# Moving the sum of squares of a second norm from TensorE to VectorE, and the scalings of its first half behind the projection

## The chip, the cores and the metric

One core of a Trainium2 chip runs the whole kernel. The metric is the device time of one execution in microseconds (us). The engines are named as the profile names them: PE is TensorE (PEld its weight loads), DVE is VectorE, ACT is ScalarE, POOL is GpSimd, SP issues the DMAs.

## What is computed

One inference step of a decoder layer, for 1024 prompt tokens and 64 sample tokens (1088 columns in all) and a model width of 1024. Cut to what matters here:

```
def rms_norm(x, g):
    xf = x.astype(jnp.float32)
    y = xf * lax.rsqrt(jnp.mean(xf * xf, axis=-1, keepdims=True) + EPS)
    return (y * g.astype(jnp.float32)).astype(x.dtype)
...
    x = x + jnp.concatenate([a, o], axis=-1) @ w_out
    h = rms_norm(x, norm_ffn_g)
    g_full = jnp.concatenate([ffn_past, h @ w_ffn_gate], axis=1)
    g = depthwise_conv_valid(g_full, ffn_conv_w, ffn_conv_b)
    x = x + (jax.nn.silu(g) * (h @ w_ffn_up)) @ w_ffn_down
```

The change lies between the first and the third of the last five lines: the end of the output projection, the norm of its result, and the operands of the feed-forward products.

## The kernel before

Everything is stored transposed: a tile holds 128 channels on the partitions and the 1088 tokens along the row. Float32 products are made of three fp32r products each: an operand is split into a high part (copied by ACT with rounding) and a low part (the rest, by a subtraction), and high x high, low x high and high x low are added up in PSUM (lines 840, 842 and 843 in the stage here).

**The last part of the output projection** (`out_half`, line 940). The projection is summed over four groups of input tiles; the last group has two tiles (`mx`, split into `mh` and `ml`, lines 858 to 864) and its weights are split into `wh` and `wl` (lines 865 to 876; `wl` on POOL, line 874). The 1088 columns are worked in two halves of 544 (`HN`). For each half, the loop runs over the eight output tiles m: `block_product` makes 12 products of 272 columns into a PSUM pair; DVE adds the pair to the residual tile `x2[m]` (line 949, called the residual addition here), SP writes that half tile to DRAM, ACT squares it (line 952), and PE sums the squares over the partitions by five products with a column of ones (line 955), all eight tiles into the one PSUM pair `ss`.

**The norm** (`norm_half`, `rstd`, line 182). From `ss`, DVE and ACT make the reciprocal root with one Newton step (`rv`, `rr`, `rt`, lines 193 to 206), PE spreads it over the partitions by five transposes (line 213), ACT copies it to `rb` (line 215). `scale` (line 960) multiplies a half tile by it. The root of the first half is made while the second half is projected.

**The feed-forward operands.** The feed-forward products use a seven-product block scheme: the blocks are the quarters of the input and their sums and differences, each split into high and low by `split` (line 880: ACT the high part, DVE the low). Block b11 is tiles 0 to 3 of the first half, b21 tiles 4 to 7 of the first half, b22 tiles 4 to 7 of the second; t1 to t4 are differences. The first products of the stage are px (b11, then b21), pv (b22), pz (t3), py (t2, t1).

**What sets the order.** Each engine works through its own queue in order. The queues are filled by a scheduler at build time, from dependences and its own guess of durations; `tc.issue_after(x)` holds an instruction back, in that order, until x. While the projection runs, the weights of the first feed-forward product are prepared too: `weight_parts` (line 899: ACT the high part, POOL the low part, line 903) and four additions on DVE (lines 918 to 921).

The rings that matter: `pair` hands out four PSUM pairs, of which `ss` holds one during a half.

## Time and profile before

| | |
|---|---|
| time, median of 3 runs | 1442.53 us (1441.99 to 1445.53) |
| profiled execution: its own time | 1442.15 us |
| profiled execution: its span | 1440.2 us |
| busy in the span: PE, DVE, ACT, POOL | 1368.0, 846.8, 515.5, 436.8 us |

The span runs from the first to the last instruction of the profiled execution; all times of the rows below are counted from its start. The execution's own time holds 1.95 us more, around the span. The stage that the change touches lies between 602 and 694 us. A row of the timeline gives the start, the time, the engine, the line of the kernel, the operation, its output and inputs, and how often it follows itself; in brackets how long the engine sat idle before it and what ended that. PEclk is the granted share of TensorE's full clock of 2.4 GHz: 1.00 is 2.4 GHz, 0.50 is 1.2 GHz.

### The profile page before, as it was taken

The numbers are of one execution on the slowest core, as the hardware profiler recorded it, in microseconds if no ns is written. First come the engines' busy times: TensorE is split into PE (matmuls) and PEld (weight loads), VectorE is DVE, ScalarE is ACT, GpSimd is POOL, SyncE is SP. The second block draws the span as 40 slices with busy tenths as digits, with TensorE's granted clock in tenths as the row PEclk, the third lists the DMA queues.
The fourth block names the chain that finished last, engine by engine and source line by source line (L and its number), as shares of the span: only waits on it lengthen the run. The fifth ranks groups of instructions, "written<-read, shape, count | busy, mean of one in ns | idle before, by whom it ended". The sixth has DMA issues, their size and how long they took to land.

```text
span 1440.2 us, 25005 instructions
## 1 busy us (share of the span) xinstructions
PE 1368.0 (95%) x10151; PEld 1298.0 (90%) x10151; DVE 846.8 (59%) x1631; ACT 515.5 (36%) x982; POOL 436.8 (30%) x307
## 2 busy tenths in 40 slices
PE   7989999999999989896999999999999999999995
PEld 7989888999977768896999999999999899999995
DVE  7398695566574566538755667556566742423146
ACT  5312111457564564235433233333323431212033
POOL 3221112110010016220554455454445312224124
PEclk9999999999999998988999999999999999999997
DMA  7237676756698795330022222122222481414003
GB/s 269 59 133 269 216 266 187 193 155 181 168 290 248 222 251 178 129 115 32 30 90 76 76 90 68 53 91 91 75 76 91 144 312 45 137 48 130 12 9 116
DMA packets 84883, 195.17 MB, mean 136 GB/s; under 512 B 12576, under 2 KB 46752, under 8 KB 84768
## 3 DMA queue, kind: packets, MB, share of 16 engines
q1 hardware_dynamic: 84768, 193.57, 42.6%
q8 instruction: 80, 1.31, 0.4%
q14 instruction: 35, 0.29, 0.1%
HBM read 145.03 MB, written 48.52 MB: 134 GB/s over the span
## 4 chain that ended last, share of the span: by engine, by line
PE 77%; DVE 11%; DMA 6%; issue 2%; POOL 1%; ACT 1%; SPq 1%; POOLq 0%; DVEq 0%; ACTq 0%
PE g L174 9%; PE g L172 9%; PE g L173 9%; PE py L840 4%; PE py L842 4%; PE py L843 4%; DVE cacc L333 4%; PE o L666 3%; PE s L581 3%; PE pz L842 3%; PE pz L843 3%; PE pz L840 3%; PE px L843 3%; PE px L840 3%; PE px L842 3%; PE t L649 2%
## 5 line engine op out<-in xcount | busy, mean ns | idle before, releaser
L148 POOL TENSOR_TENSOR wl<-wr,wh 128x768 fp32r<-128x768 f32 (+2 forms) x61 | 116.7, 1915 | 462.1 <-PE g L174 391.1
L172 PE MATMUL g<-xh,wh 128*128 128x384 f32 (+1 forms) x472 | 158.6, 336 | 0.0
L174 PE MATMUL g<-xh,wl 128*128 128x384 f32 (+1 forms) x472 | 157.1, 333 | 0.0
L173 PE MATMUL g<-xl,wh 128*128 128x384 f32 (+1 forms) x472 | 157.0, 333 | 0.0
L172 PE MATMUL g<-ah,wh 128*128 128x384 f32 (+1 forms) x432 | 141.1, 332 | 4.2 <-ACT wh L146 3.2
L173 PE MATMUL g<-al,wh 128*128 128x384 f32 (+1 forms) x432 | 143.4, 332 | 1.5 <-DVE al L1135 1.5
L174 PE MATMUL g<-ah,wl 128*128 128x384 f32 (+1 forms) x432 | 143.0, 332 | 0.5 <-POOL wl L148 0.5
L146 ACT ACTIVATE wh<-wr 128x768 fp32r<-128x768 f32 (+2 forms) x62 | 52.0, 839 | 236.2 <-PE g L174 173.9
L903 POOL TENSOR_TENSOR s<-wr,s 128x1024 fp32r<-128x1024 f32 x44 | 107.2, 2438 | 85.0 <-ACT s L902 43.2
L1157 DVE TENSOR_TENSOR x<-g,x 128x384 f32<-128x384 f32 (+1 forms) x72 | 38.0, 534 | 136.8 <-PE g L174 136.6
L622 ACT ACTIVATE y<-y,m 128x128 f32<-128x128 f32 (+1 forms) x192 | 88.4, 463 | 32.6 <-DVE m L610 32.5
L174 PEld LDWEIGHTS g<-xh,wl 128*128 128x128 f32 x472 | 89.7, 190 | 2.3 <-issue 2.1
L172 PEld LDWEIGHTS g<-xh,wh 128*128 128x128 f32 x472 | 90.0, 191 | 1.4 <-issue 1.2
L173 PEld LDWEIGHTS g<-xl,wh 128*128 128x128 f32 x472 | 90.1, 191 | 1.1 <-issue 1.0
L585 DVE CUSTOM_DVE_ANT_0 y<-s,pmk 128x128 f32<-128x128 f32 (+1 forms) x192 | 63.9, 379 | 43.2 <-PE s L581 35.8
L172 PEld LDWEIGHTS g<-ah,wh 128*128 128x128 f32 x432 | 81.7, 190 | 5.0 <-ACT wh L146 3.6
L173 PEld LDWEIGHTS g<-al,wh 128*128 128x128 f32 x432 | 81.9, 190 | 2.1 <-DVE al L1135 2.1
L174 PEld LDWEIGHTS g<-ah,wl 128*128 128x128 f32 x432 | 82.0, 190 | 0.9 <-POOL wl L148 0.9
L333 DVE SCALAR_TENSOR_TENSOR cacc<-gp,prm,cacc 128x1024 f32<-128x1024 f32 x60 | 80.1, 1334 | 0.1
L1086 DVE SCALAR_TENSOR_TENSOR fc<-gb,prm,fc 128x1104 f32<-128x1104 f32 x44 | 78.9, 1813 | 2.0 <-ACT fc L1084 1.2
L903 POOL TENSOR_TENSOR wa<-wr,wa 128x1024 fp32r<-128x1024 f32 (+1 forms) x23 | 56.1, 2442 | 61.9 <-ACT wa L902 61.9
L381 DVE TENSOR_TENSOR qkv<-g,rb 128x384 f32<-128x384 f32 (+1 forms) x53 | 41.1, 776 | 47.1 <-PE g L174 47.0
(304 smaller groups left out, 4147.0 us busy)
## 6 DMA issues: line engine op xcount, KB each, us to landing
cr<-in_kc SPq DMA_DIRECT2D x24, 768.0 KB, 8.3
cr<-in_vc SPq DMA_DIRECT2D x24, 768.0 KB, 7.5
kk<-dk SPq DMA_DIRECT2D x48, 256.0 KB, 7.6
u<-u SPq DMA_DIRECT2D x22, 544.0 KB, 3.0
ur<-u SPq DMA_DIRECT2D x22, 544.0 KB, 5.0
wr<-in_w_in SPq DMA_DIRECT2D x22, 512.0 KB, 4.9
wr<-in_w_gate SPq DMA_DIRECT2D x22, 512.0 KB, 3.3
wr<-in_w_up SPq DMA_DIRECT2D x22, 512.0 KB, 4.7
```

Source lines behind the costliest of these rows:

```text
L148: lo_eng.tensor_sub(lo, raw, hi.bitcast(F32))
L172: nc.tensor.matmul(ps[c], whi[:, k, :], xh[:, t0:t0 + n], start=(k == 0), stop=False)
L173: nc.tensor.matmul(ps[c], whi[:, k, :], xl[:, t0:t0 + n], start=False, stop=False)
L174: nc.tensor.matmul(ps[c], wlo[:, k, :], xh[:, t0:t0 + n], start=False, stop=(k == nk - 1))
L333: eng.scalar_tensor_tensor(acc[:, :S], gp[:, j:j + S], col(w0 + j), acc[:, :S], op0=ALU.mult, op1=ALU.add)
L585: nc.vector.tensor_tensor_reduce(out=y[:, o:o + n], in0=ps[:, o:o + n], in1=mask, op0=ALU.add, op1=ALU.min, scale=1.0, scalar=3e38, accum_ ...
L622: nc.scalar.activation(y, y, AF.Exp, bias=m[:, 4 * g + i:4 * g + i + 1], scale=-1.0, accum_out=den[:, g, 2 * hd + u, i:i + 1])
L840: nc.tensor.matmul(ps, whi[:, k, :], xh[:, t], start=(start and k == 0), stop=False, skip_group_check=True)
L842: nc.tensor.matmul(ps, whi[:, k, :], xl[:, t], start=False, stop=False, skip_group_check=True)
L843: nc.tensor.matmul(ps, wlo[:, k, :], xh[:, t], start=False, stop=(k == nk - 1), skip_group_check=True)
L903: nc.gpsimd.tensor_sub(lo, x, hi.bitcast(F32))
L1086: nc.vector.scalar_tensor_tensor(c[:, :W], gb[i][:, t:t + W], col(C_FW + 3 * f + t), c[:, :W], op0=ALU.mult, op1=ALU.add)
```

## The change

Three edits. (1) The squares of a half are no longer summed by PE over the partitions tile by tile: DVE adds the eight squared tiles into the first (`acc`), and PE sums the partitions once, by five products with ones in `rstd` (line 191 of the changed kernel). (2) All scalings and splits of the first half (b11 and b21) are held back behind the last residual addition; those of b21 behind the last step of the second half's root (`rooted`). The first half's norm is called after tile 3 of the second half, not after tile 2. (3) The low parts `wl` of the last group's weights are made by DVE, not by POOL (line 874).

```
-        def rstd(sq, div, new, width=N, sums=None):
+        rooted = [None]
+        def rstd(sq, div, new, width=N):
+            ps = bank(*rbank[0])
...
-            ps = sums
-            if ps is None:
-                ps = bank(*rbank[0])
-                for i, n in enumerate(size):
-                    nc.tensor.matmul(ps[:n, i:i + 1], sq[:, i * P:i * P + n], ones, start=True, stop=True)
+            for i, n in enumerate(size):
+                nc.tensor.matmul(ps[:n, i:i + 1], sq[:, i * P:i * P + n], ones, start=True, stop=True)
...
-            nc.vector.scalar_tensor_tensor(r, t, 1.5, r, op0=ALU.add, op1=ALU.mult)
+            rooted[0] = nc.vector.scalar_tensor_tensor(r, t, 1.5, r, op0=ALU.add, op1=ALU.mult).ins
...
-                nc.gpsimd.tensor_sub(lo, r, hi.bitcast(F32))
+                nc.vector.tensor_sub(lo, r, hi.bitcast(F32))
...
-            sums = pair("ss")
             for m in range(KT):
...
                 s = slot("t1", "sq", F32)
                 nc.scalar.activation(s, x, AF.Square)
-                for i in range(0, HN, P):
-                    w = min(P, HN - i)
-                    nc.tensor.matmul(sums[:w, i // P:i // P + 1], s[:, i:i + w], ones, start=(m == i == 0),
-                                     stop=(m == KT - 1), skip_group_check=True)
+                if m == 0:
+                    acc = s
+                else:
+                    added = nc.vector.tensor_add(acc, s, acc).ins
                 hook(m, added)
-            return sums, added
+            return acc, added
...
-        def first_blocks(m, added):
-            if m == 2:
-                r0.append(norm_half(sums0))
-            if m >= 4:
-                with tc.issue_after(added):
-                    scale(0, m - 4, r0[0])
-                    split(x2[m - 4][:, :HN], "b11", m - 4)
-
-        sums1, added = out_half(1, first_blocks)
-        r1 = norm_half(sums1)
-        for k in range(4):
-            with tc.issue_after(added):
-                scale(0, k + 4, r0[0])
-            split(x2[k + 4][:, :HN], "b21", k)
+        def norm_first(m, added):
+            if m == 3:
+                r0.append(norm_half(sq0))
+
+        def first_blocks(k, tag, after):
+            for i in range(k, k + 4):
+                with tc.issue_after(after):
+                    scale(0, i, r0[0])
+            for i in range(k, k + 4):
+                with tc.issue_after(after):
+                    split(x2[i][:, :HN], tag, i - k)
+
+        sq1, added = out_half(1, norm_first)
+        r1 = norm_half(sq1)
+        first_blocks(0, "b11", added)
+        first_blocks(4, "b21", rooted[0])
```

Outside the stretch between the last group of the projection and the first feed-forward products, the order of every engine stays as it was. Inside it, three places matter.

PE, around the root of the first half (g with a number above 6700 is a PSUM pair of the projection, ss the sums of squares, rr the root, sq a squared tile). Before, the last ones of the first half, where the second half has begun:

```order
L955 MATMUL ss_6701<-ones,sq_6871 128x1 x4
L955 MATMUL ss_6701<-ones,sq_6871 32x1
L955 MATMUL ss_6878<-ones,sq_6894 128x1 x4
L955 MATMUL ss_6878<-ones,sq_6894 32x1
L840 MATMUL g_6901<-mh_6628,wh_6640 128x272
```

and, 24 products later, the transposes of the root:

```order
L843 MATMUL g_6923<-mh_6634,wl_6645 128x272
L213 MATMUL g_1282_6957<-ident,rr_6949 128x128 x4
L213 MATMUL g_1283_6963<-ident,rr_6949 128x32
L955 MATMUL ss_6878<-ones,sq_6916 128x1 x4
L955 MATMUL ss_6878<-ones,sq_6916 32x1
L840 MATMUL g_6966<-mh_6628,wh_6644 128x272
```

Now, behind the 48th product of the second half (its tile 3):

```order
L843 MATMUL g_6897<-mh_6634,wl_6645 128x272
L191 MATMUL g_1278_6915<-ones,sq_6716 128x1 x4
L191 MATMUL g_1278_6915<-ones,sq_6716 32x1
L213 MATMUL g_1283_6933<-ident,rr_6925 128x128 x4
L213 MATMUL g_1284_6939<-ident,rr_6925 128x32
L840 MATMUL g_6942<-mh_6628,wh_6650 128x272
```

Fourteen of the sixteen sums with ones are gone, and no product stands between the ones of the first half and the transposes of its root.

DVE in the same place (x is a residual tile, rv, rr and rt the steps of the root). Before:

```order
L949 TENSOR_TENSOR x_1148_6214<-g_6856,x_1148_6214 128x544
L949 TENSOR_TENSOR x_1099_5934<-g_6879,x_1099_5934 128x544
L195 TENSOR_SCALAR rv_6945<-ss_6701 128x4
L198 TENSOR_SCALAR rv_6945<-ss_6701 32x1
L200 RECIPROCAL rr_6949<-rv_6945 128x5
L204 TENSOR_TENSOR rt_6952<-rr_6949 128x5
```

Now (sq_6716 is the sum of the first half, sq_6859 that of the second):

```order
L948 TENSOR_TENSOR x_1113_6014<-g_6879,x_1113_6014 128x544
L955 TENSOR_TENSOR sq_6716<-sq_6841,sq_6716 128x544
L948 TENSOR_TENSOR x_1120_6054<-g_6897,x_1120_6054 128x544
L955 TENSOR_TENSOR sq_6859<-sq_6876,sq_6859 128x544
L195 TENSOR_SCALAR rv_6921<-g_1278_6915 128x4
L198 TENSOR_SCALAR rv_6921<-g_1278_6915 32x1
L955 TENSOR_TENSOR sq_6859<-sq_6894,sq_6859 128x544
L200 RECIPROCAL rr_6925<-rv_6921 128x5
L955 TENSOR_TENSOR sq_6859<-sq_6912,sq_6859 128x544
L204 TENSOR_TENSOR rt_6928<-rr_6925 128x5
```

From the first residual addition to the root's last step, DVE's queue now holds 12 residual additions, 10 additions of squares, 2 splits `ml`, the 4 additions of lines 918 to 921 and the root's steps, one behind the other.

DVE behind the projection (b11l, b21l and b22l are low parts, rb_6932 the first half's root spread out, rb_7031 the second's). Before, all of b21 was split ahead of the second half's root:

```order
L883 TENSOR_TENSOR b11l_7093<-x_1120_6054,b11h_7092 128x544
L195 TENSOR_SCALAR rv_7096<-ss_6878 128x4
L198 TENSOR_SCALAR rv_7096<-ss_6878 32x1
L883 TENSOR_TENSOR b21l_7119<-x_1127_6094,b21h_7118 128x544
L883 TENSOR_TENSOR b21l_7124<-x_1134_6134,b21h_7123 128x544
L883 TENSOR_TENSOR b21l_7129<-x_1141_6174,b21h_7128 128x544
L883 TENSOR_TENSOR b21l_7134<-x_1148_6214,b21h_7133 128x544
L200 RECIPROCAL rr_7100<-rv_7096 128x5
```

Now the scalings of b21 stand behind that root, one split of b21 follows them, then the eight scalings of the second half (the first two shown), then the other three splits of b21 and those of b22:

```order
L206 SCALAR_TENSOR_TENSOR rr_7024<-rt_7027,rr_7024 128x5
L961 SCALAR_TENSOR_TENSOR x_1127_6094<-x_1127_6094,prm,rb_6932 128x544
L961 SCALAR_TENSOR_TENSOR x_1134_6134<-x_1134_6134,prm,rb_6932 128x544
L961 SCALAR_TENSOR_TENSOR x_1141_6174<-x_1141_6174,prm,rb_6932 128x544
L961 SCALAR_TENSOR_TENSOR x_1148_6214<-x_1148_6214,prm,rb_6932 128x544
L193 MEMSET rv_14193 128x2
L883 TENSOR_TENSOR b21l_7066<-x_1127_6094,b21h_7065 128x544
L961 SCALAR_TENSOR_TENSOR x_1127_6094<-x_1127_6094,prm,rb_7031 128x544
L961 SCALAR_TENSOR_TENSOR x_1134_6134<-x_1134_6134,prm,rb_7031 128x544
```

Of the work that lay ahead of the second half's root or beside the projection, four scalings and four splits have moved behind that root, and four scalings and four splits (b11) stand between the last residual addition and it.

At the head of the projection PE now opens four tiles at once (four products of high x high each before the first low part), where before it finished one tile first; `ss` no longer holds one of the four pairs. On ACT the high parts of the weights `s` move from behind the third and fourth square of the first half to behind the second and third of the second half; POOL's two splits `s`, each made from one of them, move with them. The four splits `wl` are gone from the head of POOL's queue, its other splits keep their order. On SP the two loads of the first up-projection weights move from behind the fourth and fifth store of a residual tile to behind the twelfth.

## Rows read from the trace of the kernel before

**Rows 1.** The page: the span, and PE's busy time.

```profile
span 1440.2 us, 25005 instructions
PE 1368.0 (95%) x10151; PEld 1298.0 (90%) x10151; DVE 846.8 (59%) x1631; ACT 515.5 (36%) x982; POOL 436.8 (30%) x307
```

**Rows 2.** Stretches of the stage: start and end, length, then busy time and number of instructions of PE, PEld, DVE, ACT and POOL, the granted clock, the DMA share and GB/s.

```profile
611.95:616.30 4.35, 4.35 (x20) 4.35 (x20) 1.77 (x3) 1.04 (x2) 2.54 (x2) 0.50 0.00 2
623.95:626.60 2.65, 2.65 (x22) 2.65 (x22) 0.72 (x1) 0.73 (x3) 0.62 (x1) 1.00 0.99 335
636.70:640.10 3.40, 3.40 (x16) 3.40 (x16) 0.35 (x3) 0.00 (x0) 0.00 (x0) 0.50 0.00 0
...
682.70:687.90 5.20, 5.20 (x23) 5.20 (x24) 5.20 (x9) 2.89 (x5) 4.72 (x2) 0.50 0.00 0
```

**Rows 3.** Who waited for whom between 585 and 705 us: total, times, longest (us).

```profile
DVE x L949 <- PE g L843: 21.3, 12, 3.0
```

**Rows 4.** The products with ones (line 955) on PE: least, median and greatest time of one in ns.

```profile
L955 PE MATMUL ss<-ones,sq x160: 164/250/373, 609.9 to 657.5; 128*128 128x1 f32 x128, 128*32 128x1 f32 x32
```

**Rows 5.** PE's timeline in the projection and at the first feed-forward products.

```profile
604.55 0.39 PE L842 MATMUL g<-ml,wh 128*128 128x272 f32 x1 [1.18 <-DVE ml L863]
...
609.92 2.06 PE L955 MATMUL ss<-ones,sq 128*128 128x1 f32 x10 [1.51 <-ACT sq L952]
611.91 0.59 PE L840 MATMUL g<-mh,wh 128*128 128x272 f32 x1
...
618.99 1.10 PE L955 MATMUL ss<-ones,sq 128*128 128x1 f32 x10
620.01 0.40 PE L840 MATMUL g<-mh,wh 128*128 128x272 f32 x1
...
634.65 2.07 PE L955 MATMUL ss<-ones,sq 128*128 128x1 f32 x10 [0.49 <-ACT sq L952]
636.65 0.59 PE L840 MATMUL g<-mh,wh 128*128 128x272 f32 x1
...
654.30 3.42 PE L955 MATMUL ss<-ones,sq 128*128 128x1 f32 x30
664.18 1.08 PE L213 MATMUL g<-ident,rr 128*128 128x128 f32 x4 [6.46 <-DVE rv L193]
...
665.44 0.59 PE L840 MATMUL px<-b11h,wa 128*128 128x272 f32 x1
```

**Rows 6.** DVE's timeline in the projection.

```profile
602.96 4.97 DVE L863 TENSOR_TENSOR ml<-mx,mh 128x544 fp32r<-128x544 f32 x3 [0.88 <-ACT mh L862]
608.45 0.72 DVE L949 TENSOR_TENSOR x<-g,x 128x544 f32<-128x544 f32 x1 [0.52 <-PE g L843]
...
614.52 0.69 DVE L918 TENSOR_TENSOR wr<-wr 128x512 f32<-128x512 f32 x1 [4.72 <-POOL w L903]
...
622.58 0.72 DVE L949 TENSOR_TENSOR x<-g,x 128x544 f32<-128x544 f32 x1 [3.04 <-PE g L843]
...
634.20 0.16 DVE L195 TENSOR_SCALAR rv<-ss 128x4 f32<-128x4 f32 x1 [0.35 <-PE ss L955]
...
636.55 0.17 DVE L206 SCALAR_TENSOR_TENSOR rr<-rt,rr 128x5 f32<-128x5 f32 x1
```

**Rows 7.** POOL's timeline: its splits in the projection.

```profile
601.42 5.93 POOL L874 TENSOR_TENSOR wl<-wr,wh 128x512 fp32r<-128x512 f32 x4 [7.76 <-ACT wh L873]
610.89 2.36 POOL L903 TENSOR_TENSOR wa<-wr,wa 128x1024 fp32r<-128x1024 f32 x1 [3.54 <-ACT wa L902]
613.20 1.29 POOL L903 TENSOR_TENSOR w<-wr,w 128x512 fp32r<-128x512 f32 x1
619.86 4.71 POOL L903 TENSOR_TENSOR s<-wr,s 128x1024 fp32r<-128x1024 f32 x2 [5.37 <-ACT s L902]
```

**Rows 8.** DVE and POOL at a later place, where a DVE operation with two inputs in SBUF meets a split of POOL (two timelines of one window), and the groups of two DVE lines and of POOL's line 903 with their least, median and greatest time in ns.

```profile
766.65 2.42 DVE L1093 TENSOR_TENSOR u<-u,fc 128x480 f32<-128x480 f32 x1
...
766.16 2.40 POOL L903 TENSOR_TENSOR s<-wr,s 128x1024 fp32r<-128x1024 f32 x1 [4.08 <-ACT s L902]
...
L1093 DVE TENSOR_TENSOR u<-u,fc x22: 654/2432/2678, 724.0 to 1146.0; 128x480 f32<-128x480 f32 x11, 128x1024 f32<-128x1024 f32 x11
...
L863 DVE TENSOR_TENSOR ml<-mx,mh x4: 715/1664/1796, 603.0 to 609.1; 128x544 fp32r<-128x544 f32 x4
...
L903 POOL TENSOR_TENSOR s<-wr,s x44: 2373/2408/3346, 619.9 to 1126.2; 128x1024 fp32r<-128x1024 f32 x44
```

**Rows 9.** ACT and DVE behind the projection.

```profile
655.78 0.66 ACT L952 ACTIVATE sq<-x 128x544 f32<-128x544 f32 x1 [0.67 <-DVE x L949]
...
660.49 2.61 DVE L883 TENSOR_TENSOR b21l<-x,b21h 128x544 fp32r<-128x544 f32 x4
663.03 0.17 DVE L200 RECIPROCAL rr<-rv 128x5 f32<-128x5 f32 x1
...
666.02 5.65 DVE L962 SCALAR_TENSOR_TENSOR x<-x,prm,rb 128x544 f32<-128x544 f32 x8 [1.98 <-ACT rb L215]
671.61 1.98 DVE L883 TENSOR_TENSOR b22l<-x,b22h 128x544 fp32r<-128x544 f32 x3
```

**Rows 10.** PE's later waits in the feed-forward's first product.

```profile
678.14 0.39 PE L840 MATMUL pz<-t3h,s 128*128 128x272 f32 x1 [1.21 <-ACT t3h L882]
682.59 0.60 PE L840 MATMUL py<-t2h,s 128*128 128x272 f32 x1 [4.05 <-ACT t2h L882]
```

More of the change, by code (lines that the diff above doesn't have):

```diff
@@ L962, in scale, with norm_half @@
             nc.vector.scalar_tensor_tensor(x, x, col(C_GFFN + k), r, op0=ALU.mult, op1=ALU.mult)
-        def norm_half(sums):
-            return rstd(None, D, lambda s: slot("t3", s, F32), HN, sums)
-        sums0, _ = out_half(0, lambda *_: None)
+        def norm_half(sq):
+            return rstd(sq, D, lambda s: slot("t3", s, F32), HN)
+        sq0, _ = out_half(0, lambda *_: None)
         r0 = []
-        def first_blocks(m, added):
-            if m == 2:
-                r0.append(norm_half(sums0))
-            if m >= 4:
-                with tc.issue_after(added):
-                    scale(0, m - 4, r0[0])
-                    split(x2[m - 4][:, :HN], "b11", m - 4)
-        sums1, added = out_half(1, first_blocks)
-        r1 = norm_half(sums1)
-        for k in range(4):
-            with tc.issue_after(added):
-                scale(0, k + 4, r0[0])
-            split(x2[k + 4][:, :HN], "b21", k)
+        def norm_first(m, added):
[12 more added lines that the diff above has]
+        first_blocks(4, "b21", rooted[0])
         for k in range(4):
```

## The prediction

> **What bounds the kernel now.** The page comes first [rows 1]: PE is busy for 95% of the span, so a change counts by what it takes off PE's path, or puts on it. Second, the list of waits for the stage [rows 3]: in the projection DVE's residual additions wait for PE, 21.3 us in all. PE sets the pace there, and what PE no longer does is gained until another engine becomes the slower one. Third, PE's timeline [rows 5]. The reader is to see the groups of ones between the products: ten rows of one column each, which hold PE from 618.99 to 620.01, 1.03 us, at the full clock, and twice 2.0 us at the lower one (609.92 to 611.91, 634.65 to 636.65), both with a wait ahead (1.51 and 0.49 us). The 160 rows [rows 4] are 16 groups; three stand behind the last product (654.30), so 13 lie inside the projection: 11 x 1.03 + 2 x 2.0 + 2.0 of waits = 17.3 us. Fourth, the granted clock [rows 2]: 2.4 GHz in most of the stage (1.00 at 623.95), 1.2 GHz (0.50) behind the opening waits (20 products up to 616.30), behind the two groups of ones with a wait at 634 (16 products), and behind PE's 4.05 us wait [rows 10]. A product takes 0.125 us at 2.4 GHz (22 in 2.65 us, with the edges) and 0.226 at 1.2 (23 in 5.20 us). Fifth, behind the projection: PE waits 6.46 us for the second root [rows 5], DVE works through scalings and splits [rows 9], and PE waits for DVE's results up to py at 682.59 [rows 10]. From 666 on DVE is the bound (busy for all of 682.70 to 687.90 too [rows 2]); behind that PE is again, for the rest of the kernel.
>
> **The change, part by part.** The sum is made against the profiled execution, 1442.15 us (span 1440.2 and 1.95 around it), 0.4 us under the median of 1442.53.
>
> *Opening.* Before, two of the splits ml beside POOL's wl took some 1.66 us each; alone one takes 0.715 [rows 6 to 8]. Three of them from 602.96 took 4.97 us, so the second ended at 606.2. Now DVE makes wl itself: from 602.08, when it was free (602.96 less the 0.88 idle), three of some 0.61 us (0.69 at 614.52, less the overlap), then ml, wl, ml at 0.635 an operation of 544 columns (b21's four end in 2.61 us, of which 0.07 is the last one's tail [rows 9]) end at 605.8: the move costs nothing. Eight more products make the first tile: first residual addition at 607.3, against 608.45 [rows 6].
>
> *The first root.* PE could make the 12 tiles up to it in 144 x 0.125 = 18 us from 604.5, so by 622.5, and with 29 products at 1.2 GHz by 625.4. DVE is later: in its queue, between the first residual addition and the root's last step, stand 12 residual additions, 10 additions of squares and 2 ml, 24 x 0.635 = 15.2; four additions of 512 columns, 2.4; the root's six steps of 0.16, 0.9 [rows 6]. That is 18.5 us, so 625.8, if nothing holds DVE up.
>
> POOL does. The row at 766.65 shows a DVE addition of 480 columns that takes 2.42 us instead of 0.65: it ends 0.5 us after POOL's split that began at 766.16 and took 2.40 [rows 8]. Of the 22 of this line half took over 2.4 us. A DVE operation with two SBUF inputs thus waits for POOL's running split; residual additions, with one input in PSUM, do not (0.72 at 622.58, in the middle of the splits s from 619.86 [rows 6, 7]). Additions of squares have two SBUF inputs. This speaks against the change: the Trainium skill, GPSIMD Engine Reference, section Key points, says that GpSimd shares its SBUF interfaces with VectorE and contends with DVE instructions that have two SBUF inputs. By that rule the adds are not as cheap as DVE's idle share suggests, and the trace agrees (2.42 against 0.65). Four splits lie in this stretch [rows 7]: 2.36, 1.29 and two of 2.36. The first two meet adds that are spread out: half, 1.8. The two s are met by adds that follow each other in the root's chain: whole, less one residual addition each, 3.4. Together 5.2; ends 0 and 8.4. So the first root is done at 631.0 (ends 626 and 634), PE, done with its ones a microsecond after its products, stands from 624 or 626 to then, and the transposes follow.
>
> *The second half's rest.* Transposes 1.26 us (664.18 to 665.44), then 48 products. PE has stood, so the clock will be low; I take the longer of the two recoveries in the trace, 20 products: 20 x 0.226 + 28 x 0.125 = 8.0. The last product ends at 640.3, where 654.3 stood: **14.0 us gained**. Ends: all high 6.0, all low 10.9.
>
> *Behind the projection*, on DVE, counted from the last product: residual addition, ACT's square (0.66 [rows 9]), two semaphore steps and the last addition of squares 2.3; four scalings at 0.70 (5.65 for eight) 2.8; rv 0.14; three splits 1.9; reciprocal 0.2; a split 0.64; root 0.55; four scalings 2.8; a split and a memset 0.7; eight scalings 5.6; three splits 1.9. Total 19.5, at b22's first split; before, 671.61 - 654.30 = 17.3. So **2.2 us lost**: two additions, three scalings and two splits more on this path, against the 1.98 us for which DVE waited for rb. PE's ten ones fit beside the four scalings, and the five transposes and rb beside the moved four. From b22 on DVE's order is as before. PE now waits for b21 before px can end, 2 to 3 us, and must make some 36 products after it, 8.1 us at 1.2 GHz; the last b21 at 19.5 plus 8.1 is 27.6, and py's t2, which PE waited for, comes at 28.3 + 2.2. The 4.05 us wait [rows 10] is the cover; without it this would cost 2 to 3.
>
> *Nothing* for the later loads on SP: the up-projection weights are used behind 682, their loads now some 630. The feed-forward keeps its order and PE its bound, so what is gained stays.
>
> Sum: -14.0 + 2.2 = -11.8, so 1442.15 - 11.8 = **1430.4 us**.
>
> **The rivals.**
>
> *No meeting with POOL* (the splits fall between the adds). Then PE and DVE both reach the first root at 626, and with the clock high the projection ends at 633: some 1424. For: rows beside POOL with 0.65. Against: two 2.36 us splits come right where squares queue.
>
> *POOL in full and a low clock.* All four splits met (8.4) and 48 products at 1.2 GHz (10.9): +3.2 + 2.9, 1436.5. For: the s row reaches 3.35 us [rows 8].
>
> *DVE's round trip is the pace.* If each addition of squares waited for its own tile's square, a tile would cost 0.72 + 0.66 + 0.64 and two steps, 2.1 us; 16 tiles, 34, and with the opening (4.3), the root and lines 918 to 921 (3.3), ml (1.3) and POOL (5.2) the projection needs 48 of its old 51 us, and 2.2 are lost behind it: 1441. Against: the order puts a later tile's residual addition between them.
>
> *No overlap between DVE operations.* The Trainium skill, VectorE: DVE Perf Modes, section The DRAIN you can't avoid, has the next operation start only when the pipe of the one ahead is empty. As a mechanism here, in rows: each operation would cost its whole 0.72 us, not 0.635; 24 ahead of the root and some 24 behind the projection make 48 x 0.085 = 4.1 more, 1434.5. Against: four splits of 0.70 end in 2.61 us [rows 9].
>
> *Slower: PE starves at the first root and stays slow.* Place: the transposes right behind the ones. If all four splits fall into DVE's chain, the three long ones at the longest row's 3.35, it is 11.3 instead of 5.2, 6.1 more; a clock at 1.2 GHz from there to py costs 28 products more in the projection and 72 behind it, 10.1: together 16.2 against 11.8, 1446.6. It decides once the halt and the slow products take 12 us more than in my sum. Against: a split holds at most one add, there are few splits, and the trace's clock came back after 16 and 20 dense products.
>
> **How the numbers follow.** Forecast 0.59, no meeting 0.12, POOL in full 0.13, round trip 0.08, no overlap 0.04, slower 0.04. The forecast's own bounds (clock 6.0 to 10.9, POOL 0 to 8.4) are 1424 to 1437; with the cases on either side, 8 in 10 lie from 1425 to 1438. A measurement of this kernel tells 0.3%, 4.3 us, from no change: faster means under 1438.2. Faster 0.59 + 0.12 + 0.13 + 0.04, less 0.01 for tails, 0.87; same 0.09; slower 0.04.
>
> **What would show it.** Line 955's sums on PE gone, two groups of ones left; ml at 0.72; a wait of PE of 5 to 8 us before the first transposes, put down to DVE; additions of squares of 1.5 to 3 us there, beside POOL's s; PE's last product of the projection near 640, the first of px near 650, b22's first split near 660, py's t2 near 671 with a wait of about 4 us ahead; from there every row 11 to 12 us earlier. Wrong: if PE's halt is over 15 us, if DVE sits idle waiting for ACT's squares, or if the gap between the last product and py grows beyond 31 us.

## The result, and the profile after

The changed kernel takes 1427.88 us (median of 4 runs, 1426.11 to 1432.72) beside 1443.03 for the kernel before on the same chip: a ratio of 0.9898, 95% interval 0.987 to 0.9925. A second comparison, of 8 runs with 23 of before, gives 0.9919 (0.9895 to 0.9943), 11.7 us of 1441.88.

Single executions differ by 10 us and more, so the runs alone cannot tell 2 us; the traces can. Most of that variation lies ahead of the stage that was changed: the last 320-column product of the attention's output starts at 603.35 us in the first trace of the changed kernel and at 592.11 in the second, with the same order of instructions, and the two spans differ by 11.4 us. So everything below is counted from that product (601.24 in the trace of before), and **"the stage"** is the time from there to py's first product, behind which PE is the bound again. The landmarks:

| kernel (one trace each) | first residual addition | first root, last step begins | last projection product ends | second root, last step begins | px begins | py begins = stage |
|---|---|---|---|---|---|---|
| before | 7.21 | 35.31 | 53.21 | 62.63 | 64.20 | **81.35** |
| changed | 6.16 | 29.57 | 39.25 | 47.29 | 48.86 | **69.27** |
| changed, second trace | 6.15 | 29.58 | 38.40 | 46.44 | 48.01 | **68.42** |

The stage is 12.1 and 12.9 us shorter. Behind it the trace of before has 757.61 us left, those of the changed kernel 758.28 and 758.97: these traces show nothing given back later and nothing more gained there. That part of the kernel varies too: over the 14 traces of all experiments it takes 755.30 to 762.91 us, and in two traces of one kernel 757.58 and 762.91, so a few us there would not show.

The page of the changed kernel, against [rows 1]:

```profile
span 1430.9 us, 24745 instructions
...
PE 1350.0 (94%) x10011; PEld 1280.5 (89%) x10011; DVE 861.0 (60%) x1649; ACT 514.3 (36%) x982; POOL 431.5 (30%) x303
```

PE has 140 instructions fewer (160 products with ones gone, 20 for the two groups left) and 18 us less busy time. The waits between 585 and 705 us, where [rows 3] had DVE waiting for PE 12 times:

```profile
DVE x L948 <- PE g L843: 6.8, 3, 4.5
...
PE g L213 <- DVE rv L193: 5.8, 1, 5.8
```

DVE's 21.3 us have shrunk to 6.8, in three waits, and PE now waits for DVE instead: the bound has moved. PE's timeline, against [rows 5, 10]:

```profile
603.35 0.31 PE L174 MATMUL g<-mh,wl 128*128 128x320 f32 x1
...
626.25 1.18 PE L191 MATMUL g<-ones,sq 128*128 128x1 f32 x10 [1.73 <-DVE sq L955]
633.24 1.33 PE L213 MATMUL g<-ident,rr 128*128 128x128 f32 x5 [5.81 <-DVE rv L193]
...
644.96 1.60 PE L191 MATMUL g<-ones,sq 128*128 128x1 f32 x10 [2.37 <-DVE sq L955]
650.95 1.33 PE L213 MATMUL g<-ident,rr 128*128 128x128 f32 x5 [4.38 <-DVE rr L206]
652.21 0.59 PE L840 MATMUL px<-b11h,wa 128*128 128x272 f32 x1
...
660.49 0.40 PE L842 MATMUL px<-b21l,wa 128*128 128x272 f32 x1 [1.98 <-DVE b21l L883]
...
672.62 0.51 PE L840 MATMUL py<-t2h,s 128*128 128x272 f32 x1 [4.05 <-ACT t2h L882]
```

Two groups of ones are left, and PE stands 7.5 us in two pieces ahead of the first root's transposes. DVE's timeline and POOL's for the same stretch, against [rows 6, 7]:

```profile
609.51 0.72 DVE L948 TENSOR_TENSOR x<-g,x 128x544 f32<-128x544 f32 x1 [1.64 <-PE g L843]
...
613.32 1.67 DVE L955 TENSOR_TENSOR sq<-sq,sq 128x544 f32<-128x544 f32 x1
...
615.55 1.18 DVE L955 TENSOR_TENSOR sq<-sq,sq 128x544 f32<-128x544 f32 x1
...
626.66 2.34 DVE L955 TENSOR_TENSOR sq<-sq,sq 128x544 f32<-128x544 f32 x1
...
629.11 2.67 DVE L955 TENSOR_TENSOR sq<-sq,sq 128x544 f32<-128x544 f32 x1
...
632.92 0.17 DVE L206 SCALAR_TENSOR_TENSOR rr<-rt,rr 128x5 f32<-128x5 f32 x1
```

```profile
611.96 2.45 POOL L903 TENSOR_TENSOR wa<-wr,wa 128x1024 fp32r<-128x1024 f32 x1 [16.19 <-ACT wa L902]
614.36 1.79 POOL L903 TENSOR_TENSOR w<-wr,w 128x512 fp32r<-128x512 f32 x1
626.07 5.14 POOL L903 TENSOR_TENSOR s<-wr,s 128x1024 fp32r<-128x1024 f32 x2 [9.91 <-ACT s L902]
```

No row of DVE's timeline between 609.51 and 632.92 has a wait ahead of it: DVE is busy through the whole stretch. Four of the additions of squares take 1.67, 1.18, 2.34 and 2.67 us, each beside a split of POOL (such a pair is called a meeting below); the other six ahead of the root take 0.71 to 0.73. Over 0.715 us an addition, the four meetings make 0.95 + 0.46 + 1.62 + 1.95 = 5.0 us.

### The profile page after: what moved, and what is told of

Its sections match the earlier page's. It is cut to its first block, busy times and chain, and to the rows that moved or that the text cites. A ratio compares the mean times of both kernels' runs of the same rounds, so it can differ in the third digit from the quotient of the medians.

```text
span 1430.9 us, 24745 instructions
## 1 busy us (share of the span) xinstructions
PE 1350.0 (94%) x10011; PEld 1280.5 (89%) x10011; DVE 861.0 (60%) x1649; ACT 514.3 (36%) x982; POOL 431.5 (30%) x303
## 3 DMA queue, kind: packets, MB, share of 16 engines
q8 instruction: 79, 1.29, 0.4%
## 4 chain that ended last, share of the span: by engine, by line
PE 76%; DVE 12%; DMA 6%; issue 2%; POOL 1%; ACT 1%; SPq 1%; POOLq 0%; ACTq 0%; DVEq 0%
PE g L174 9%; PE g L172 9%; PE g L173 9%; PE py L840 4%; PE py L842 4%; PE py L843 4%; DVE cacc L333 4%; PE o L666 3%; PE s L581 3%; PE pz L843 3%; PE pz L842 3%; PE pz L840 3%; PE px L843 3%; PE px L840 3%; PE px L842 3%; PE t L649 3%
```

## Experiments

All are timed against the kernel before on the same chip (ratio with its 95% interval), but judged by the stage of their one trace.

**The changed kernel again.** No edit.

> The changed kernel once more, for a second trace. In its first trace the stage from the last 320-column product of the attention's output to py's first product was 12.0 us shorter than before, while the medians differ by 15.2 us. Theory: the change is worth what the stage shows, so this trace has 12 us again (11 to 13), the first root's last step 28 to 30 us behind the time at which DVE is free for the stage, PE's wait ahead of the first transposes 5 to 6.5 us; the rest of the difference lies ahead of the stage and varies from run to run, median 1427 to 1431. Rival: some 3 us more are gained behind py; then the stretch from py's first product to the end is 3 us shorter than in the trace of before, in this trace as well.

Its figures stand in the table: stage 12.9 us shorter, root 29.58, PE's wait 5.16, 758.97 us behind py (before 757.61). The gain is in the stage, and the rival falls: neither trace gains 3 us behind py. The medians of the two comparisons lie 15.2 and 14.1 us apart, while the ratios make 14.7 and 11.7 us; the stage's 12 to 13 lies within that, and the time ahead of the stage alone varies from 592.11 to 605.46 us over all traces.

### Which edit gives what

**Only wl on DVE** (edit 3 alone, on the kernel before):

```diff
-                nc.gpsimd.tensor_sub(lo, r, hi.bitcast(F32))
+                nc.vector.tensor_sub(lo, r, hi.bitcast(F32))
```

> Before, with the low parts wl made on DVE and nothing else changed. Theory (the gain is the sums' that left PE): 0 to 0.5 us faster, 1442.5 to 1443.0; the splits ml fall from 1.66 to 0.72 us, PE's products with ones stay 160. Rival (the opening, where splits met POOL, was the loss): 3 us or more faster, under 1440.

Ratio 1.0001 (0.998 to 1.0023): nothing, within what the runs tell; the rival falls. The stage of its trace was 83.20, 1.9 longer, because of a further low-clock stretch inside the projection, which the trace of before has not. It begins at groups of ones, on PE's timeline:

```profile
621.39 1.10 PE L955 MATMUL ss<-ones,sq 128*128 128x1 f32 x10
...
622.78 0.28 PE L842 MATMUL g<-ml,wh 128*128 128x272 f32 x1
622.90 0.38 PE L843 MATMUL g<-mh,wl 128*128 128x272 f32 x1
623.09 0.43 PE L840 MATMUL g<-mh,wh 128*128 128x272 f32 x1
623.31 1.89 PE L955 MATMUL ss<-ones,sq 128*128 128x1 f32 x10
```

PE had not waited; from 623.09 on its products take 0.43 instead of 0.28 us and the next ones 1.89 instead of 1.10. The same happens in two more experiments below.

**Only the scalings behind the projection** (edit 2 alone, on the kernel before: the first half's root behind the fourth tile, its scalings and splits moved as in the change, the sums left on PE).

```diff
-            if m == 2:
+            if m == 3:
                 r0.append(norm_half(sums0))
-            if m >= 4:
-                with tc.issue_after(added):
-                    scale(0, m - 4, r0[0])
-                split(x2[m - 4][:, :HN], "b11", m - 4)
...
+        first_blocks(0, "b11", added)
+        first_blocks(4, "b21", rooted[0])
...
```

> Before, with the sums left on PE and the first half's scalings and splits moved behind the projection. Theory: the projection's PE path keeps its 16 groups of ones, so its last product stays within 1.5 us of where it was, and the work moved is paid for behind it: 2 to 5 us slower, 1445 to 1448. Rival (the moved scalings are the gain, since they stood in front of residual additions for which PE waited): 5 us or more faster, under 1438.

1446.36 us, ratio 1.0031 (1.0013 to 1.0049), stage 85.55: 4.2 longer. The size is as expected and the rival falls, but not by the expected way: the last product came at 56.60, 3.4 us later (at most 1.5 expected), through another such stretch (a granted clock of 0.60 from 646 to 652, where before 645 to 651 has 1.00) behind two groups of ones at 643.56 and 644.76, again without a wait of PE, and with a 14th group of ones ahead of the last product, where before had 13; the work behind the projection (last product to px 8.55 us against 10.99, px to py 20.40 against 17.15) took 0.8 more.

**The changed kernel without edit 2** (scalings and splits beside the projection again, the sums on DVE):

```diff
-            if m == 3:
-                r0.append(norm_half(sq0))
+            if m == 2:
+                r0.append(norm_half(sq0))
+            if m >= 4:
+                with tc.issue_after(added):
+                    scale(0, m - 4, r0[0])
+                split(x2[m - 4][:, :HN], "b11", m - 4)
...
```

> The changed kernel, with the first half's scalings and splits put back beside the projection (the root behind the third tile of the second half, scalings from the fifth). Theory: eight DVE operations of 0.64 us, 5.1 us, stand in a queue that already sets the pace, so the last product of the projection comes 4 to 6 us later than in the changed kernel, and of that the shorter work behind the projection gives 2 to 4 back: 1 to 4 us over the changed kernel, 1429 to 1432. Rival one (moving them only cost, as the 2.2 us term has it): 2 us under the changed kernel, 1426 or less. Rival two (the move is most of the gain): 8 us or more over it, 1436 and up.

1428.68 us (0.3 under the expected range), ratio 0.9925 (0.9898 to 0.9952), stage 71.19: 1.9 to 2.8 over the changed kernel. Rivals one and two fall. The price stood in another place than expected: the last product came at 39.36, almost unmoved, but the second root at 52.47 instead of 47.29 and 46.44, 5.2 to 6.0 later, since the scalings in DVE's queue held up the last squares; from that root to py it took 18.72 instead of 21.98, 3.3 back. So by these single traces the sums' move gives 10.2 us of the stage (81.35 to 71.19, with edit 3 and whatever the opening's clock adds, see below), and edit 2, a loss by itself, gives another 2 to 3 once DVE is the bound.

**The changed kernel without edit 3** (the first diff in reverse).

> The changed kernel with the low parts wl of the projection's weights made on POOL again, nothing else changed. Theory (the move of wl neither costs nor gives): stage 68 to 71, first residual addition some 1 us later than in the changed kernel (7.2 instead of 6.15 behind the last 320-column product), median 1427 to 1430. Rival (wl on DVE costs, as the 1.9 us longer stage of the kernel with this edit alone would have it): stage 66.5 to 67.5.

1432.42 us, ratio 0.993 (0.9902 to 0.9958), stage 72.04: the median 2.4 and the stage 1.0 over the expected range. The first residual addition came 1.5 us late, but not by POOL: in this trace the granted clock fell to 0.50 right behind the opening (16 products from 603.60 to 606.80), and DVE waited 2.68 us for PE there. That fall comes and goes between traces of one kernel; between the two of the late transposes (below) it makes 1.55 us. Less that, the stage would be 70.5, an estimate: inside the range, but still 1.2 to 2.1 over the changed kernel. The rival, that wl on DVE costs, falls; that wl on POOL costs nothing is not shown.

### What a group of ones costs

**Each product with ones twice**, on the kernel before; the divisor is doubled, the result stays:

```diff
-                    nc.tensor.matmul(sums[:w, i // P:i // P + 1], s[:, i:i + w], ones, start=(m == i == 0),
+                    for d in range(2):
+                        nc.tensor.matmul(sums[:w, i // P:i // P + 1], s[:, i:i + w], ones, start=(m == i == d == 0),
...
```

> Before, with each product of squares and ones issued twice into the same sum and the divisor doubled, so that PE makes 20 instead of 10 in each group. Theory (a group holds PE for 1.03 us at the full clock and 2.0 at the lower): 13 groups inside the projection add 13 to 17 us up to its last product (53.21 before), less at most 2 of waits ahead of two groups; the stage 93 to 99, the median 1454 to 1460. Rival (the groups stand where PE waits for DVE anyway, and the 17.3 us are mostly cover): under 8 us, 1450 or less.

1472.01 us, ratio 1.0208 (1.0173 to 1.0242), stage 108.74: 27.4 longer, the last product 28.0. The rival (ones beside waits) falls, and the theory is 10 us short. PE's timeline and then the stretches around one of its rows say why (after the start and end: length, busy time of PE, PEld, DVE, ACT and POOL with their instructions, granted clock, DMA share, GB/s):

```profile
624.69 0.29 PE L842 MATMUL g<-ml,wh 128*128 128x272 f32 x1
624.81 8.41 PE L956 MATMUL ss<-ones,sq 128*128 128x1 f32 x60
633.15 0.59 PE L843 MATMUL g<-mh,wl 128*128 128x272 f32 x1
```

```profile
621.00:624.80 3.80, 3.80 (x30) 3.80 (x30) 2.35 (x4) 3.26 (x5) 1.66 (x1) 0.95 0.37 146
629.00:633.20 4.20, 4.20 (x26) 4.14 (x26) 0.00 (x0) 1.14 (x2) 2.50 (x2) 0.50 0.34 120
633.20:636.00 2.80, 2.80 (x13) 2.80 (x13) 0.72 (x1) 0.66 (x1) 0.00 (x0) 0.50 0.00 0
```

One row holds three groups: 60 one-column products, 8.41 us, with PE never idle, and the granted clock falls from 0.95 (mostly 2.4 GHz) to 0.50 (1.2 GHz) inside it and stays there for the products behind. Inside the projection the ones now take 39.2 us (7 such rows of 20 to 60 from 613.65 to 675.33, 280 products in all: 14 groups of 20) where before 13 groups of 10 had 11 x 1.03 + 2 x 2.0 = 15.3: 23.9 more, and the remaining 4.1 of the 28.0 are mostly products at the lower clock. So ones cost PE more than their time at the full clock: here PE dropped to 1.2 GHz without having stood. That ones bring this about is the reading of these rows; no run puts other small products in their place.

### POOL's splits

**No splits on POOL** for the first gate's weights: their low parts are set to zero, so that these products lack them.

```diff
-            nc.gpsimd.tensor_sub(lo, x, hi.bitcast(F32))
+            if bare:
+                nc.gpsimd.memset(lo.bitcast(F32), 0.0)
+            else:
+                nc.gpsimd.tensor_sub(lo, x, hi.bitcast(F32))
...
```

> The changed kernel with the low parts of the first gate's weights (w, wa and the two s) set to zero by POOL instead of being split off, so these products lack their low part; POOL's instructions stay in their places but read nothing. The stage is counted from the last 320-column product of the attention's output to py's first product: 81.35 us in the trace of before, 69.27 and 68.42 in the two of the changed kernel, where the first root's last step comes at 29.6. Theory (additions of squares wait for POOL's running split, 5.0 us in all): additions all at 0.7 us, the root's last step at 24.5 to 25.5, PE's wait ahead of the transposes under 2 us, the stage 62 to 65, the median 5 to 7 us under the changed kernel's. Rival one (the meetings are free, since another wait takes their place): root at 28 or later, stage 68 to 70. Rival two (a POOL instruction that only writes holds DVE as long): additions still 1.5 us and more.

1424.31 us, ratio 0.9893 (0.9862 to 0.9924), root 27.26, stage 67.10. POOL's writes of zeros, which wait for no input, had run before the additions of squares (the last at 597.96, 0.95 us), so no addition met one. But the last ran beside DVE's first split wl, which has two inputs in SBUF: from 598.28 that split took 0.68 us, as in the trace of the changed kernel, where POOL stood at that time. That one overlap speaks against rival two. The squares' additions take 0.72, so POOL's splits were what lengthened them. That is the place of the rule which the Trainium skill, GPSIMD Engine Reference, section Key points, gives (GpSimd's contention, at the SBUF interfaces that it shares with VectorE, with DVE instructions that have two SBUF inputs); the traces agree, 2.34 and 2.67 us beside a split, 0.72 without. But of the 5.0 us only 2.3 come back at the root, half of what theory expected, and 1.3 to 2.2 in the stage, where it expected 62 to 65; PE still waited 3.05 us ahead of the transposes. DVE's timeline at the root:

```profile
617.23 0.73 DVE L952 TENSOR_TENSOR x<-g,x 128x544 f32<-128x544 f32 x1 [0.28 <-PE g L843]
...
619.37 2.82 DVE L959 TENSOR_TENSOR sq<-sq,sq 128x544 f32<-128x544 f32 x4
...
623.99 0.56 DVE L204 TENSOR_TENSOR rt<-rr 128x5 f32<-128x5 f32 x1 [1.46 <-ACT rr L201]
624.59 0.17 DVE L205 SCALAR_TENSOR_TENSOR rt<-rt,rv 128x5 f32<-128x5 f32 x1
624.79 0.17 DVE L206 SCALAR_TENSOR_TENSOR rr<-rt,rr 128x5 f32<-128x5 f32 x1
```

With the meetings gone the waits that they had covered come to light: 0.28 for PE, 1.46 for ACT's square root, small gaps, and the root's own steps, which had stood between slow additions. The result lies between theory and rival one, and part of rival one is thus true.

**The two splits s on DVE.**

```diff
-            nc.gpsimd.tensor_sub(lo, x, hi.bitcast(F32))
+            (eng or nc.gpsimd).tensor_sub(lo, x, hi.bitcast(F32))
...
+        first_gate = blocks_of_first(first_gate) + blocks_of_both(first_gate, nc.vector)
```

> The changed kernel with the two splits s of the first gate's weights made by DVE instead of POOL, nothing else changed. By 0.705 us for 544 columns one takes some 1.25, so 2.5 us more stand in DVE's queue ahead of the first root, while the two additions that met them on POOL lose 3.6 us. Theory: root 0.5 to 1.5 us earlier than in the changed kernel (28.1 to 29.1 behind the last 320-column product), stage 67 to 68.7. Rival (the meetings with POOL cost nothing that the queue would not have waited for anyway): root 2.5 later, 32, stage 71 to 72.

1427.27 us, ratio 0.9905 (0.9874 to 0.9937), root 28.03, stage 67.15. A split takes 1.21 us on DVE; 3.6 of meetings less 2.4 is 1.2 us, and the root came 1.5 earlier. The rival (root at 32) falls. The stage is that of the run without any of the four splits on POOL, 67.10.

### PE's halt at the transposes

**The first root two tiles later.**

```diff
-            if m == 3:
+            if m == 5:
                 r0.append(norm_half(sq0))
```

> The changed kernel with the first root's transposes issued two tiles later, behind the sixth tile of the second half, so that PE has 24 more products before it needs DVE. Theory (DVE's queue, not PE's halt, is the bound): PE's wait of 5.8 us ahead of the transposes shrinks to under 4 us or splits into waits for additions, the last product of the projection (39.25 and 38.40 behind the last 320-column product) moves by less than 1.5 us either way, the stage stays at 67.5 to 70.5. Rival (the halt and the low clock behind it are the loss, some 5.8 + 1.8 us): last product at 32 to 35, stage 62 to 65.

1429.51 us, ratio 0.9925 (0.9897 to 0.9954), stage 71.69, last product 40.98. The rival (stage 62 to 65) falls, but my figures missed too: the wait did not shrink, it grew to 9.63 us. PE had finished its 14 tiles at 621.97, 24.0 us into the stage, while DVE, with two more tiles in its queue, reached the root's last step at 33.40, 3.8 later than in the changed kernel. DVE is the bound up to the root, so PE's products cannot fill the halt. Even the root's tiny steps now met POOL, as DVE's timeline and POOL's show:

```profile
630.11 1.23 DVE L205 SCALAR_TENSOR_TENSOR rt<-rt,rv 128x5 f32<-128x5 f32 x1
631.37 1.18 DVE L206 SCALAR_TENSOR_TENSOR rr<-rt,rr 128x5 f32<-128x5 f32 x1
```

```profile
629.96 2.58 POOL L903 TENSOR_TENSOR wa<-wr,wa 128x512 fp32r<-128x512 f32 x2 [4.08 <-ACT wa L902]
```

**The transposes late**: the root is computed where the change has it, and only PE's five transposes and the spreading of rb are issued behind the last tile.

```diff
...
             if m == 3:
-                r0.append(norm_half(sq0))
+                r0.append(norm_half(sq0, True))
+            if m == 7:
+                r0.append(r0.pop()())
```

(rstd returns the transposes and the copies to rb as a function, called at m == 7.)

> The changed kernel, with the first root computed where it is, but its five transposes and the spreading of rb issued behind the last tile of the second half instead of behind the fourth, so that PE's queue does not stop at them. Stage counted from the last 320-column product to py's first product: 69.27 and 68.42 in the changed kernel's two traces, last product of the projection at 39.25 and 38.40, root at 29.6. Theory: PE's halt of 5.2 to 5.8 us at the transposes goes, and the last product comes 5 to 8 us earlier, at 31 to 34; DVE's queue up to the root is as long as before (root at 29 to 30), and behind it six additions of squares, four residual additions and the scalings still follow each other, so only what DVE then idled (4.5 us) comes back: stage 64 to 66, the median 3 to 5 us under the changed kernel's. Rival one (DVE's queue is the bound throughout, PE's halt costs nothing): stage 68 to 70. Rival two (all of PE's gain is carried on): stage 61 to 63.

1426.14 us, ratio 0.9891 (0.9854 to 0.9927), last product 31.82, root 31.68, stage 65.61: stage and last product as expected, the root 1.6 us late by a fall of the clock at the opening, the median 1.6 under the changed kernel's (taken on another chip) instead of 3 to 5. Once more:

> The kernel with the late transposes once more. In its first trace the granted clock fell to 0.50 some 4 us behind the last 320-column product, as it did before the change but in neither trace of the changed kernel, and the first residual addition came 1.5 us later than there (7.67 instead of 6.16); the stage was 65.61 us. Theory (the late transposes give some 4 us, and the fall at the opening, which this edit does not touch, took 1.5 of it): with the opening at 2.4 GHz a stage of 63.5 to 64.8, with the fall 65 to 66.2. Rival (the gain in the first trace was variation): stage over 67.5.

1423.43 us, ratio 0.9872 (0.9839 to 0.9906); no fall at the opening, root 30.13, last product 30.27, stage 64.06. The stages bear the theory out, and the rivals of both runs fall. Behind py this trace took 762.91 us, the first one of the same kernel 757.58 and the changed kernel 758.28 and 758.97; with 5.3 us between two traces of one kernel, these cannot show whether some of the gain is given back there. The stretches of 10 us from 616.13 on, 20 us into the stage of the second trace:

```profile
616.13:626.13 10.00, 8.24 (x68) 8.02 (x66) 9.99 (x15) 5.55 (x8) 5.21 (x2) 1.00 0.46 165
626.13:636.13 10.00, 3.10 (x18) 2.56 (x16) 9.86 (x19) 6.64 (x12) 3.38 (x2) 0.79 0.51 165
636.13:646.13 10.00, 6.04 (x32) 5.46 (x33) 9.93 (x20) 6.22 (x12) 0.00 (x0) 0.69 0.00 1
646.13:656.13 10.00, 8.44 (x48) 7.39 (x47) 10.00 (x16) 3.55 (x6) 0.00 (x0) 0.83 0.01 2
```

DVE (third) is now busy for 39.79 of 40 us. The last product came 8 to 9 us earlier than in the changed kernel, the stage only 4.4 to 5.2 shorter at the same opening: about as much as DVE's longest wait for PE in the changed kernel's two traces, 4.5 and 4.2 us. PE's halt did not cost its own length; it cost what DVE stood behind the root until PE, restarted at 1.2 GHz, had a tile for it.

**Both together**, late transposes and s on DVE.

> The late transposes together with the two splits s on DVE (1.21 us each there, against 2.4 and 2.7 us for the additions that met them on POOL). With the late transposes DVE is busy throughout, so what leaves its queue should come back in full. Theory: two meetings less two splits, 3.6 - 2.4 = 1.2 us, the first root 1.2 to 1.6 earlier, stage 0.8 to 1.8 under that of the late transposes alone at the same opening: 62.3 to 64 at 2.4 GHz, 63.8 to 65 with the fall. Rival (the second root's wait for the last square, or the root's own steps, take the place): no change, within 0.5.

1426.64 us, ratio 0.9887 (0.9852 to 0.9922), stage 64.06 again: the rival holds, and my reason fails. DVE's timeline:

```profile
633.56 0.14 DVE L204 TENSOR_TENSOR rt<-rr 128x5 f32<-128x5 f32 x1
...
635.85 1.22 DVE L205 SCALAR_TENSOR_TENSOR rt<-rt,rv 128x5 f32<-128x5 f32 x1
...
638.26 0.15 DVE L206 SCALAR_TENSOR_TENSOR rr<-rt,rr 128x5 f32<-128x5 f32 x1
...
640.39 2.87 DVE L966 SCALAR_TENSOR_TENSOR x<-x,prm,rb 128x544 f32<-128x544 f32 x4 [0.40 <-ACT rb L217]
```

The order that resulted put the root's last steps between later additions, so the root's last step began at 33.64 instead of 30.13, PE waited 3.68 us for it at the transposes, and the scalings waited for rb.

By the stage the late transposes are the best version, 4.4 to 5.2 us under the changed kernel at the same opening. By the runs, 0.9872 and 0.9891 against 0.9898 and 0.9919, the intervals overlap.

## Why the prediction was right

The forecast's mechanism and its sum held: -11.8 us expected, 12.1 and 12.9 in the stage. By its own steps, as distances from the same product:

- *Opening, no cost*: first residual addition expected at 607.3, which is 6.1 behind; 6.16 and 6.15 came. What the step did not have: the opening's fall to 1.2 GHz, in the trace of before [rows 2], is in neither trace of the changed kernel. The step's eight products at the full clock were thus partly luck: in a trace with the fall the first residual addition comes at 7.67. All four traces with the sums on PE show the fall, and two of the ten with the sums on DVE, so it may in part be an effect of the change; no run separates that. Between the two traces of the late transposes it makes 65.61 - 64.06 = 1.55 us of the stage.
- *First root at 631.0, end of its last step*: 29.8 expected, 29.7 came. The queue's 18.5 us and 5.2 for POOL stand against 23.6 measured from the first residual addition, 5.0 of it meetings. PE's wait ahead of the transposes, 5 to 8 us, was 5.81 and 5.16.
- *Second half's rest*: 20 slow products and the last one at 39.1 expected; 18 slow ones and 39.25 came in the first trace, 9 and 38.40 in the second. 14.0 us gained, 14.0 and 14.8 measured.
- *Behind the projection*: 19.5 expected from the last product to b22's first split, 19.0 in both traces, against 17.2 before by the same reading: 1.9 lost instead of 2.2.
- *Cover*: py's wait for t2 is 4.05 us as before, so PE's slow px products behind b21 (a wait of 1.98 and 2.15) stayed hidden.
- *Rivals*: PE did starve, but far from the 12 us over the sum at which that rival decides; the late transposes put what it cost at 4.4 to 5.2 us. POOL's meetings came in full beside the two s and in part beside the others, 5.0 us and not 8.4. Up to the first root DVE's queue had no gap, so its round trip did not set the pace. "No overlap" fell as well: three splits in a row end in 1.99 us, starts 0.635 apart, where one takes 0.72. The Trainium skill, VectorE: DVE Perf Modes, section The DRAIN you can't avoid, has the next operation wait for an empty pipe, and adds that one which is not held starts earlier; the splits agree with the second. Additions that follow each other into the same sum come nearer to the first, four in 2.82 us, 0.70 apart.

Two of its readings were too simple. The price of the meetings with POOL, 5.2 us, was right as a count of what DVE lost, but not as what their absence gives: the rival without them put the time 6 us lower, and the run without the splits shows 1.3 to 2.2 in the stage.

And the ones' price, 17.3 us, was taken as their time on PE's path and the waits ahead of two groups; the clock that falls with them belongs to it. From the last 320-column product to the last product of the projection, PE's rows in the trace of before and the first of the changed kernel add up, from start to start, to 15.8 and 1.2 us of ones, 30.7 and 26.7 us for the same 192 products, 0.7 and 1.3 us of transposes, and 5.7 and 9.8 us of standing. So the 14.0 us gained are 14.6 of ones and 4.0 of products at a higher clock, less 4.1 of standing and 0.6 of transposes. How many of the slow products before were the ones' doing stays open, since most of them stand in the opening, behind waits. The low clock at 634, which the prediction puts behind a wait of 0.49 us, began ahead of that wait: the group at 632.92 took 1.24 instead of 1.10 us, and from 633.50 to 634.16 the granted clock was 0.61 with PE busy. With edit 2 alone two groups at 633.33 took 3.79 us without any wait.

Two smaller readings were off, without effect on the sum: three of the splits ml, not two, ran beside wl before (1.54, 1.79 and 1.80 us), and the 22 additions of line 1093 have two widths, of each of which nine in eleven were lengthened (0.65 to 2.43 us at 480 columns, 1.22 to 2.67 at 1024).

## What to carry to other kernels

When work moves from the bound to an idle engine, add up that engine's queue to the next point where the bound waits for it; here that sum, with the lengthening beside POOL, gave the root's time within 0.1 us where the opening ran at the full clock. What removing a delay gives must be asked anew, since other waits may lie under it. And where two engines wait for each other in turn, ask which of the two stands behind the meeting point: issuing the five transposes later brought the last product 8 us forward, and the stage only about as much as DVE had stood.

## What the runs showed of the hardware

- The granted clock can fall while PE is never idle: inside 60 one-column products (8.41 us) it went from 0.95 to 0.50, and in the kernels with edit 3 alone and edit 2 alone it fell at single groups of ten between products (0.28 to 0.43 us a product).
- Whether it falls behind the opening's waits (1.43 and 0.8 us) differs between traces of one kernel: at one execution of the late transposes it was 0.50 (603 to 605), at the other 1.00 (599.80 to 601.80). What decides it stays open.
- Beside a split of POOL even a DVE operation of 5 columns with two inputs in SBUF takes 1.2 us instead of 0.17. The meeting can lengthen POOL's split too: w, begun at 614.36 in the changed kernel while an addition of squares was running, takes 1.79 us, where before it took 1.29 without one.
